# Keeping the split weights of two projections in DRAM between three passes of a hybrid encoder block

## The chip, the cores and the metric

The kernel runs on one core of one Trainium2 chip. The metric is the device time of one execution in microseconds (us). The profile is one further execution, recorded by the hardware profiler.

## The reference

The block handles 1024 tokens of width 1024 in float32. Stick-breaking attention (8 heads of 64) and mLSTM (4 heads of 128) run side by side, their outputs are joined and go through one output projection; then a PEER layer routes each token to 128 of 16384 single-neuron experts through a query projection. Cut to what matters here:

```python
x = x + gate1 * jnp.einsum('bsm,md->bsd', mixed, w_out[l])          # 1024 x 1024 weights
h2 = rms_norm(x, g_norm2[l]) * (1 + scale2) + shift2
# peer(h2, ...)
q = jnp.einsum('bsd,dq->bsq', h, w_q).reshape(b, s_len, 8, 2, 128)   # 1024 x 2048 weights
scores = jnp.einsum('bshpc,hpnc->bshpn', q, sub_keys)
top_s, top_i = lax.top_k(scores, 16)
# pairs of the two top lists, top 16 of them, softmax gate, then
act = gelu(einsum('td,tkd->tk', xb, expert_u[idx]))
y = einsum('tk,tkd->td', gate * act, expert_v[idx])
```

## The kernel before

Tokens are columns. Matrix products that need float32 accuracy use three matmuls of a rounded type (F32R): each operand is split into a high part (ACT copies it with rounding, L121) and a low part (VectorE or POOL subtracts, L125), and `mm3` sums high x high, low x high and high x low (L129 to L131).

`weights` (L257 to L269) makes the two parts of one block of 128 output features, `wh` and `wl`, each 128 x 8 x 128 (0.524 MB), each with two buffers. In the stages considered here it works in four quarters: a load of 128 KB on SP's queue into `wf` (L266, three buffers), an ACT copy into `wh`, a POOL subtraction into `wl`. The output projection has 8 such blocks, the query projection 16.

The tokens are taken in three groups, `GROUPS`: 512, 256 and 256. For each group the output projection (`out_proj`, blocks named `wo`) and the routing (`route`, blocks named `wq`, product tile `pq`) run once, so each weight block is loaded and split three times. Around these, `build` weaves generators together by hand-set step weights:

- attention of the later tokens (`stick_on`, `mlstm`), with keys and values streamed back on SP's queue (`kvrs`, `kvrm`), beside the first output projection, the first routing, the second output projection and the start of the second routing;
- the gate matrix build (`wbuild`, tiles `wo1`, `wo2`, `wm`, `wst`, product `wps`) beside the third output projection and third routing. Its tile `wo` in the rows without a suffix on a VectorE or ACT line L984 to L989 belongs to this build, not to the output projection;
- 24 blocks of the dense expert products made ahead (`ahead`, tiles `uf`, `uh`, `ul`, `da`) from the third routing on.

Last comes the dense phase: 128 expert blocks for 640 tokens on TensorE, woven with row gathers for the other 384 tokens, issued on POOL's queue (tiles `gu`, `gv`, five buffers, L918 and L929).

The weave gives the order in which instructions are written; a scheduler that times the program in a simulation then settles each engine's order. Each engine and each DMA queue works in that order: an instruction that waits holds all behind it.

In DRAM the kernel already keeps intermediate tiles (`mix_d`, `x1_d`, `kvs_d` and others) in the pool `dr`.

Of the kernel before, what the change touches and what calls it, by code (L numbers as in the profile page):

```python
# [8 lines left out]
F32 = mybir.dt.float32  # L9
F32R = mybir.dt.float32r  # L10
# [7 lines left out]
P = 128  # L18
S = 1024
D = 1024  # L20
KB = D // P
# [91 lines left out]
class Kernel:  # L113
# [140 lines left out]
        nc.vector.tensor_mul(y, y, t)  # L254
        return y

    def weights(self, src, name, pool=None):  # L257
        w = pool or self.wp
        wh = w.tile([P, KB, 128], F32R, tag="wh", name=f"wh{name}", bufs=2)
        wl = w.tile([P, KB, 128], F32R, tag="wl", name=f"wl{name}", bufs=2)  # L260

        n, e = (4, "v") if w is self.wp else (2, "g")
        for q in range(KB // n):
            ks = slice(n * q, n * q + n)
            wf = w.tile([P, n, 128], F32, tag="wf", name=f"wf{name}_{q}", bufs=3)
            self.nc.sync.dma_start(wf, src[:, ks])  # L266
            self.split(wf, wh[:, ks], wl[:, ks], "s", e)
        return wh, wl

    def start(self, hp, st):  # L270
# [412 lines left out]
    def out_proj(self, f, w):  # L683

        nc, a, pp = self.nc, self.a, self.pp
        t0, n = GROUPS[f]
        gl = slice(t0, t0 + n)
        mx = self.wide(f, "mx")
        for k in range(KB):
            v = w.tile([P, n], F32, tag="kst", name=f"mx{f}_{k}", bufs=4)  # L690
            nc.sync.dma_start(v, self.mix_d[f][k])
            if k >= 4:
                o = w.tile([P, n], F32, tag="rq", name=f"mo{f}_{k}", bufs=2)
                nc.sync.dma_start(o, self.o_d[k - 4][:, gl])
                nc.vector.tensor_mul(v, v, o)
            self.split(v, mx[0][:, k], mx[1][:, k], "s", "v")
        yield 7
        acc = w.tile([P, n], F32, tag="acc", name=f"acc{f}", bufs=1)
        for i in range(KB):
            wt = self.weights(a["w_out"][i], f"wo{f}_{i}", w)  # L700
            ps = pp.tile([P, H], F32, tag="mm", name=f"op{f}_{i}")[:, :n]
            self.product(ps, wt, mx)
            x1 = w.tile([P, n], F32, tag="kst", name=f"xr{f}_{i}", bufs=4)
            nc.sync.dma_start(x1, a["xT"][:, i, gl])
            nc.vector.scalar_tensor_tensor(out=x1, in0=ps, scalar=self.mod[:, 16 + i : 17 + i], in1=x1, op0=ALU.mult,
                                           op1=ALU.add)
            nc.sync.dma_start(self.x1_d[i][:, gl], x1)
            if i:
                sq = w.tile([P, n], F32, tag="sq", name=f"sqh{f}_{i}", bufs=1)
                nc.scalar.activation(sq, x1, AF.Square)  # L710
                nc.gpsimd.tensor_add(acc, acc, sq)
            else:
                nc.scalar.activation(acc, x1, AF.Square)
            if not f:
                self.to_tokens(i, x1, self.x1t_d, w)
            yield 6
        yield None
        ms = pp.tile([P, H], F32, tag="mm", name=f"msh{f}")[:, :n]
        nc.tensor.matmul(ms, self.mean1024, acc, start=True, stop=True)
        r = self.rsqrt_wide(ms, f"h{f}", n, w, n)  # L720
        h2 = [x[:, :, ND0:] for x in self.da] if f == 1 else self.wide(f, "h2")
        for k in range(KB):
            u = w.tile([P, n], F32, tag="kst", name=f"h2{f}_{k}", bufs=4)
            nc.sync.dma_start(u, self.x1_d[k][:, gl])
            nc.vector.scalar_tensor_tensor(out=u, in0=u, scalar=self.scol2[:, k : k + 1], in1=r, op0=ALU.mult,
                                           op1=ALU.mult)
            sh = self.mod[:, 24 + k : 25 + k]
            self.shifted(u, sh, h2[0][:, k], h2[1][:, k])
            if not f:
                nc.scalar.activation(u, u, AF.Identity, bias=sh)  # L730
                self.to_tokens(k, u, self.h2_d, w)
                nc.sync.dma_start(self.h2e_d[k], u[:, G:])
            yield 5
        self.h2[f] = h2
# [29 lines left out]
    def route(self, f, w):  # L764

        nc, a, pp = self.nc, self.a, self.pp
        n = GROUPS[f][1]
        nt = n // P

        nh = max(1, 4 // nt)  # L770
        for hp in range(16):
            if hp % (2 * nh) == 0:
                top = w.tile([P, nh * nt, 2, 16], F32, tag="top", name=f"top{f}_{hp}", bufs=2)
                tix = w.tile([P, nh * nt, 2, 16], U32, tag="tix", name=f"tix{f}_{hp}", bufs=2)
            r0 = hp // 2 % nh * nt
            nm = f"{f}_{hp}"
            wt = self.weights(a["w_q"][hp], f"wq{f}_{hp}", w)
            sk = w.tile([P, P], F32, tag="sk", name=f"sk{nm}", bufs=2)
            nc.sync.dma_start(sk, a["skT"][:, hp])
            ps = pp.tile([P, H], F32, tag="mm", name=f"pq{nm}")[:, :n]  # L780
            self.product(ps, wt, self.h2[f])
            q = w.tile([P, n], F32, tag="rq", name=f"rq{nm}", bufs=2)
            nc.scalar.copy(q, ps)
            sc = pp.tile([P, H], F32, tag=SC_TAG[f], name=f"sc{nm}")
            for i in range(nt):
                ts = slice(i * P, (i + 1) * P)
                nc.tensor.matmul(sc[:, ts], q[:, ts], sk, start=True, stop=True)
            self.best([sc[:, i * P : (i + 1) * P] for i in range(nt)], [top[:, r0 + i, hp % 2] for i in range(nt)],
                      [tix[:, r0 + i, hp % 2] for i in range(nt)], "mr", nm, w)
            yield 9  # L790
            if hp % 2:
                if r0 + nt == nh * nt:
                    self.level2(f, hp // 2 + 1 - nh, nh, top, tix, w)
                if hp == 15:
                    self.softmax(f, w)
                yield 11
# [298 lines left out]
    def build(self):  # L1095
        tc, nc, ctx, a = self.tc, self.nc, self.ctx, self.a
        self.early_c = ExitStack()
        self.consts()
        pool = lambda n, b, **kw: ctx.enter_context(tc.tile_pool(name=n, bufs=b, **kw))
        dr = pool("dr", 1, space=bass.MemoryType.DRAM)  # L1100
        tiles = lambda nm, n, shape: [dr.tile(shape, F32, name=f"{nm}{i}") for i in range(n)]
        self.o_d, self.mix_d = tiles("o_d", 4, [P, S]), [tiles(f"mix_d{f}_", KB, [P, g[1]]) for f, g in enumerate(GROUPS)]
        self.kvs_d, self.kvm_d = tiles("kvs_d", 4, [P, NT, 2, P]), tiles("kvm_d", 4, [P, NT, 2, P])
# [14 lines left out]
        with ExitStack() as st:  # L1118
            open_ = lambda n: st.enter_context(tc.tile_pool(name=n, bufs=1, reuse_waits="tile"))
            mp = open_("mp")  # L1120
            hp = open_("hp")
# [32 lines left out]
        def queries(u):  # L1154

            return woven(*((chain(*(f(h, u) for h in range(4))), 1) for f in (self.stick_on, self.mlstm)))
# [10 lines left out]
        with right("xw") as xw:  # L1167
            project = lambda f: self.out_proj(f, xw)
            route = lambda f: self.route(f, xw)
            with right("ak3") as self.ak:  # L1170
                q = [queries(1), queries(2)]
                with left("bg") as self.bg:
                    p = project(0)
                    run(woven((chain(upto(p), upto(p)), 95), attend(q[0], CUT[0])))
                    r = route(0)
                    run(woven((islice(r, CUT[1]), 10 * CUT[1]), attend(q[0], 56 - CUT[0])))
                    p = project(1)
                    run(woven((r, 10 * (24 - CUT[1])), (upto(p), 55), attend(q[1], CUT[2])))
                self.da = [enter(left(f"da{x}")).tile([P, KB, ND - 256], F32R, name=f"da{x}") for x in "hl"]
                r = chain(self.early(xw), p, route(1))  # L1180
                run(woven((islice(r, CUT[3] + 9), 10 * CUT[3] + 45), attend(q[1], 72 - CUT[2])))
# [16 lines left out]

            before = ahead()
            run(woven((first(route(2)), 240), (wbs(*W_T[1]), 1.8 * 32 * len(W_T[1])), (islice(before, N_A[0]), 6 * N_A[0])))  # L1200
        self.early_c.close()
        self.wr = enter(right("wr"))
# [74 lines left out]
```

## Time and profile before

| | |
|---|---|
| median of 3 runs | 3305.99 us (3305.73 to 3321.35) |
| the profiled execution | 3304.93 us |
| its span, first to last instruction | 3303.2 us |
| TensorE's mean granted clock in it | 0.961 of full speed |
| busy share of the span | PE 93%, VectorE 82%, ACT 51%, POOL 46% |
| DMA queues by share of 16 engines | SP's queue 35.4%, POOL's queue 34.0% |

PE is TensorE's matmuls, PEld its weight loads, DVE VectorE, POOL GpSimd, SP the engine that issues most DMAs. Matmuls are pipelined and their ends are modelled, so a busy PE is not PE at its peak. "L125" is line 125 of the kernel. Busy shares are means over stages with different limits, so the stages have to be read apart.

### The profile page before, as it was taken

How to read it: one execution, taken by the hardware profiler on the slowest of the kernel's cores; microseconds unless marked ns; L12 is line 12 of the kernel's file. 1: busy time of each engine (PE TensorE's matmuls, PEld its weight loads, DVE VectorE, ACT ScalarE, POOL GpSimd, SP SyncE). 2: the span in 40 equal slices, each digit the busy share in tenths (PEclk: the TensorE clock that was granted, in tenths of full speed). 3: DMA queues.
4: the chain of work that ended last, by engine and by line, in shares of the span. 5: the costliest groups of instructions: out<-in, count | busy, mean ns of one | idle time of the engine just before them, and what ended most of it. 6: DMA issues, size and time to landing. Idle time of an engine off the chain costs nothing.

```text
span 3303.2 us, 53461 instructions
## 1 busy us (share of the span) xinstructions
PE 3060.2 (93%) x18581; PEld 2790.1 (84%) x18581; DVE 2696.0 (82%) x5464; ACT 1678.0 (51%) x3646; POOL 1534.7 (46%) x1334
## 2 busy tenths in 40 slices
PE   6998998988889789999889999999999998999995
PEld 4666676666667679999889999999999998999995
DVE  7776764479988966988679898988888888888997
ACT  4766776774676696789323333333333333333331
POOL 3000003645676434243356565556555555555564
PEclk8999998989989889999999999999999999999998
DMA  5244334532333455398989999999999998899998
GB/s 188 77 131 141 104 89 161 162 114 81 94 115 101 139 192 170 138 333 329 335 302 334 338 326 334 332 341 329 335 314 333 334 315 314 306 339 330 321 333 280
DMA packets 388863, 799.51 MB, mean 242 GB/s; under 512 B 35032, under 2 KB 216792, under 8 KB 386032
## 3 DMA queue, kind: packets, MB, share of 16 engines
q1 hardware_dynamic: 268368, 387.03, 35.4%
q0 software_dynamic: 110624, 402.77, 34.0%
q10 hardware_dynamic: 9600, 6.29, 0.6%
q8 instruction: 146, 2.39, 0.3%
q14 instruction: 125, 1.02, 0.1%
HBM read 716.23 MB, written 79.73 MB: 241 GB/s over the span
## 4 chain that ended last, share of the span: by engine, by line
PE 28%; issue 11%; DVE 11%; DMA 11%; POOL 8%; ACT 4%; SPq 0%; POOLq 0%; DVEq 0%; ACTq 0%
POOL gv L929 4%; PE da L129 4%; PE da L131 4%; PE da L130 4%; DMA vf<-in_V_dram 3%; POOL gu L918 3%; DMA gu<-in_U_dram,idx 2%; PE dy L129 2%; PE dy L130 2%; PE dy L131 2%; PE wps L998 2%; DVE gy L931 2%; PE yr L129 1%; PE yr L130 1%; PE yr L131 1%
## 5 line engine op out<-in xcount | busy, mean ns | idle before, releaser
L918 POOL DMA_INDIRECT gu<-in_U_dram,idx x384 | 521.4, 1358 | 455.9 <-DVE gu L920 373.6
L929 POOL DMA_INDIRECT gv<-in_V_dram,idx x384 | 528.7, 1377 | 367.6 <-DVE gy L931 316.3
L931 DVE SCALAR_TENSOR_TENSOR gy<-gv,gA,gy 128x1024 f32<-128x1024 f32 x384 | 491.1, 1279 | 15.0 <-DMA gv<-in_V_dram,idx 12.5
L920 DVE SCALAR_TENSOR_TENSOR gu<-gu,gh 128x1024 f32<-128x1024 f32 x384 | 460.2, 1220 | 43.0 <-DMA gu<-in_U_dram,idx 38.5
L1092 ACT COPY dt<-dy 128x384 f32<-128x384 f32 x336 | 159.9, 480 | 497.4 <-PE dy L131 425.1
L129 PE MATMUL dy<-dgh,vh 128*128 128x384 f32 x1024 | 345.6, 339 | 18.0 <-ACT dt L1092 18.0
L129 PE MATMUL da<-dah,uh 128*128 128x384 f32 x1024 | 347.5, 339 | 8.9 <-ACT uh L121 6.1
L131 PE MATMUL da<-dah,ul 128*128 128x384 f32 x1024 | 346.7, 339 | 1.1 <-DVE ul L125 1.1
L130 PE MATMUL da<-dal,uh 128*128 128x384 f32 x1024 | 346.8, 339 | 0.0
L130 PE MATMUL dy<-dgl,vh 128*128 128x384 f32 x1024 | 344.9, 337 | 0.0
L131 PE MATMUL dy<-dgh,vl 128*128 128x384 f32 x1024 | 344.1, 337 | 0.0
L129 PE MATMUL yr<-dgh,vh 128*128 128x256 f32 x1024 | 283.3, 285 | 17.1 <-ACT vh L121 15.4
L129 PE MATMUL da<-h2h,uh 128*128 128x256 f32 x1024 | 291.4, 285 | 0.0
L130 PE MATMUL da<-h2l,uh 128*128 128x256 f32 x1024 | 290.9, 284 | 0.0
L131 PE MATMUL da<-h2h,ul 128*128 128x256 f32 x1024 | 290.7, 284 | 0.0
L130 PE MATMUL yr<-dgl,vh 128*128 128x256 f32 x1024 | 287.3, 284 | 0.6 <-DVE dgl L125 0.6
L131 PE MATMUL yr<-dgh,vl 128*128 128x256 f32 x1024 | 281.7, 283 | 0.0
L125 POOL TENSOR_TENSOR vlm<-kvrm,vhm 128x128 fp32r<-128x128 f32 x56 | 31.1, 557 | 448.5 <-ACT vhm L121 438.4
L1093 DVE TENSOR_TENSOR dy<-dy,dt 128x384 f32<-128x384 f32 x336 | 184.6, 553 | 52.1 <-ACT dt L1092 48.4
L125 DVE TENSOR_TENSOR vl<-vf,vh 128x1024 fp32r<-128x1024 f32 x128 | 156.2, 1220 | 84.6 <-ACT vh L121 82.9
L125 POOL TENSOR_TENSOR wlwq<-wfwq,whwq 128x256 fp32r<-128x256 f32 x192 | 149.6, 796 | 135.7 <-ACT whwq L121 130.5
L129 PEld LDWEIGHTS dy<-dgh,vh 128*128 128x128 f32 x1024 | 194.2, 190 | 21.0 <-ACT dt L1092 21.0
(435 smaller groups left out, 8927.1 us busy)
## 6 DMA issues: line engine op xcount, KB each, us to landing
uf<-in_UT_dram SPq DMA_DIRECT2D x128, 512.0 KB
vf<-in_V_dram SPq DMA_DIRECT2D x128, 512.0 KB
w_d<-wst SPq DMA_DIRECT2D x19, 2048.0 KB
dw<-w_d SPq DMA_DIRECT2D x32, 1216.0 KB
wfwq<-in_w_q_dram SPq DMA_DIRECT2D x192, 128.0 KB
wada<-in_w_adaT_dram SPq DMA_DIRECT2D x64, 256.0 KB
wfwo<-in_w_out_dram SPq DMA_DIRECT2D x96, 128.0 KB
wada<-in_w_adaT_dram SPq DMA_DIRECT2D x16, 512.0 KB
```

Of the source, the lines that this page charges most:

```text
L125: e.tensor_sub(lo, src, hi.bitcast(F32))
L129: mm(out, sh, mh, start=start, stop=False, skip_group_check=skip)
L130: mm(out, sh, ml, start=False, stop=False, skip_group_check=skip)
L131: mm(out, sl, mh, start=False, stop=stop, skip_group_check=skip)
L918: nc.gpsimd.indirect_dma_start(out=u, out_offset=None, in_=a["U"], in_offset=bass.IndirectOffsetOnAxis(ap=idx[:, k : k + 1], axis=0))
L920: nc.vector.scalar_tensor_tensor(out=u, in0=u, scalar=1.0, in1=h2, op0=ALU.mult, op1=ALU.mult, accum_out=A[:, k : k + 1])
L929: nc.gpsimd.indirect_dma_start(out=vv, out_offset=None, in_=a["V"], in_offset=bass.IndirectOffsetOnAxis(ap=idx[:, k : k + 1], axis=0))
L931: nc.vector.scalar_tensor_tensor(out=y, in0=vv, scalar=A[:, k : k + 1], in1=y, op0=ALU.mult, op1=ALU.add)
L998: nc.tensor.matmul(ps[:, t], o2[:, t], ms[t], start=True, stop=True)
L1092: nc.scalar.copy(t, ps)
L1093: nc.vector.tensor_add(y[:, i], y[:, i], t)
```

## The change

The first time that a weight block of the output or the query projection is made, both finished parts are also stored to DRAM, in tiles of their own, on SP's queue. In the two later passes the block is not loaded and split again: its two parts are loaded from DRAM straight into `wh` and `wl`, with two transfers of 0.524 MB on POOL's queue. The other users of `weights` pass no name to keep and do as before. The five buffers of the gathers (`GU`) are the same before and after.

```diff
-    def weights(self, src, name, pool=None):
+    def weights(self, src, name, pool=None, keep=None):
+
         w = pool or self.wp
         wh = w.tile([P, KB, 128], F32R, tag="wh", name=f"wh{name}", bufs=2)
         wl = w.tile([P, KB, 128], F32R, tag="wl", name=f"wl{name}", bufs=2)
+        if keep in self.parts_d:
+            for t, d in zip((wh, wl), self.parts_d[keep]):
+                self.nc.gpsimd.dma_start(t, d.bitcast(F32R))
+            return wh, wl
 
         n, e = (4, "v") if w is self.wp else (2, "g")
         for q in range(KB // n):
...
             self.nc.sync.dma_start(wf, src[:, ks])
             self.split(wf, wh[:, ks], wl[:, ks], "s", e)
+        if keep:
+            self.parts_d[keep] = [self.dr.tile([P, KB, 128], F32, name=f"{x}_{keep}") for x in ("kwh", "kwl")]
+            for t, d in zip((wh, wl), self.parts_d[keep]):
+                self.nc.sync.dma_start(d, t.bitcast(F32))
         return wh, wl
...
-            wt = self.weights(a["w_out"][i], f"wo{f}_{i}", w)
+            wt = self.weights(a["w_out"][i], f"wo{f}_{i}", w, f"o{i}")
...
-            wt = self.weights(a["w_q"][hp], f"wq{f}_{hp}", w)
+            wt = self.weights(a["w_q"][hp], f"wq{f}_{hp}", w, f"q{hp}")
...
-        dr = pool("dr", 1, space=bass.MemoryType.DRAM)
+        dr = self.dr = pool("dr", 1, space=bass.MemoryType.DRAM)
+        self.parts_d = {}
```

## Rows read from the trace of the kernel before

**Rows 1.** The page: busy time of each engine, its share of the span, instructions.
```profile
PE 3060.2 (93%) x18581; PEld 2790.1 (84%) x18581; DVE 2696.0 (82%) x5464; ACT 1678.0 (51%) x3646; POOL 1534.7 (46%) x1334
```

**Rows 2.** Windows of two phases: length, engines' busy us, granted clock, DMA share, GB/s.
```profile
535.00:1410.00 875.00, 774.04 (x4261) 631.13 (x4262) 705.23 (x2592) 623.57 (x1661) 451.96 (x517) 0.92 0.43 138
1410.00:3303.00 1893.00, 1816.91 (x12338) 1809.33 (x12336) 1628.78 (x2145) 704.87 (x1309) 1052.36 (x770) 0.98 0.93 325
```

**Rows 3.** Windows by stage, columns as named in the first line.
```profile
core 0: us, PE busy (x) PEld busy (x) DVE busy (x) ACT busy (x) POOL busy (x), PEclk, DMA share, GB/s
550.00:640.00 90.00, 88.98 (x398) 64.75 (x397) 43.13 (x75) 66.89 (x172) 63.61 (x77) 0.99 0.61 186
640.00:880.00 240.00, 206.01 (x904) 149.10 (x904) 214.27 (x954) 146.30 (x364) 119.50 (x136) 0.92 0.33 98
880.00:975.00 95.00, 84.89 (x401) 59.89 (x401) 86.02 (x257) 66.70 (x182) 74.40 (x91) 0.91 0.42 123
975.00:1110.00 135.00, 115.35 (x665) 93.02 (x666) 124.68 (x511) 85.19 (x221) 89.18 (x102) 0.92 0.34 104
1110.00:1160.00 50.00, 38.66 (x230) 36.02 (x230) 45.46 (x128) 44.35 (x129) 18.42 (x18) 0.81 0.45 147
1160.00:1240.00 80.00, 67.15 (x452) 62.06 (x450) 51.91 (x98) 80.00 (x238) 23.14 (x27) 0.89 0.53 193
1240.00:1280.00 40.00, 37.57 (x272) 36.78 (x272) 13.89 (x66) 24.40 (x65) 21.54 (x28) 0.96 0.40 124
1280.00:1350.00 70.00, 67.28 (x502) 66.47 (x501) 62.19 (x265) 47.49 (x134) 31.21 (x32) 0.98 0.53 188
```

**Rows 4.** The chain that ended last, 1160 to 1240 us, its shares by line.
```profile
by line: ACT wm L994 46.9%; ACT wst L999 21.4%; ACT wo L985 7.4%; ACT wo L984 6.8%; ACT whwo L121 4.6%; ACT h2h L308 4.0%; ACT whwq L121 3.0%; issue 2.6%; ACT sqh L710 1.9%; ACT rwyh L248 0.7%; ACT rwth L251 0.6%; ACT rwyh L249 0.4%
```

**Rows 5.** The same chain, 975 to 1110 us.
```profile
by line: DMA wfwq<-in_w_q_dram 12.6%; issue 5.4%; POOL wlwq L125 4.4%; DVE L L507 4.1%; PE pq L130 3.5%; DVE mr L809 3.4%; PE pq L129 3.4%; PE pq L131 3.2%; PE sc L787 3.1%; DVE xs L895 2.7%; PE y L138 2.4%; DVE top L805 2.3%; DVE tix L807 
```

**Rows 6.** The same chain, 1240 to 1280 us: shares, then pieces (start, us).
```profile
by line: DMA wfwq<-in_w_q_dram 35.3%; POOL wlwq L125 13.5%; ACT whwq L121 7.6%; PE da L129 6.7%; PE da L130 6.5%; PE da L131 6.0%; issue 4.6%; PE sc L787 4.2%; PE wps L998 2.9%; PE pq L129 2.6%; PE pq L130 2.6%; ACT uh L121 2.4%; PE pq L131
...
1254.12 2.33 DMA wfwq<-in_w_q_dram
...
1266.45 2.74 DMA wfwq<-in_w_q_dram
...
1274.04 2.15 DMA wfwq<-in_w_q_dram
```

**Rows 7.** Groups of instructions, 535 to 1410 us: busy us, mean ns; idle before them.
```profile
L125 POOL TENSOR_TENSOR wlwq<-wfwq,whwq 128x256 fp32r<-128x256 f32 x192 | 149.6, 796 | 135.7 <-ACT whwq L121 130.5 <-PE wps L998 4.8
...
L125 POOL TENSOR_TENSOR wlwo<-wfwo,whwo 128x256 fp32r<-128x256 f32 x96 | 81.3, 861 | 61.9 <-ACT whwo L121 40.3 <-PE wps L998 19.7 <-PE op L131 0.7
L121 ACT CAST whwq<-wfwq 128x256 fp32r<-128x256 f32 x192 | 73.2, 409 | 63.1 <-DMA wfwq<-in_w_q_dram 49.9 <-PE pq L130 9.6 <-PE op L130 2.3
...
L121 ACT CAST whwo<-wfwo 128x256 fp32r<-128x256 f32 x96 | 36.7, 406 | 24.9 <-DMA wfwo<-in_w_out_dram 22.2 <-PE op L130 1.9 <-issue 0.5
```

**Rows 8.** Windows of tile wfwo (two rows), then wfwq: ACT, POOL busy us.
```profile
1110.00:1160.00 50.00, 5.30 (x14) 11.31 (x14) 0.81 0.45 147
1160.00:1240.00 80.00, 4.64 (x12) 13.32 (x14) 0.89 0.53 193
...
1160.00:1240.00 80.00, 3.33 (x8) 6.14 (x8) 0.89 0.53 193
```

**Rows 9.** Issues by POOL, whole span: ns min/median/max of one.
```profile
L918 POOL DMA_INDIRECT gu<-in_U_dram,idx x384: 932/1312/1990, 1411.8 to 2987.4; - x192
...
L1049 POOL DMA_DIRECT2D dw<-we_d x1: 606/606/606, 1589.8 to 1589.8; - x1
```

**Rows 10.** Issues of the query weights by SP's queue, ns min/median/max.
```profile
L266 SPq DMA_DIRECT2D wfwq<-in_w_q_dram x192: 327/328/1546, 618.8 to 1341.5; - x192
```

**Rows 11.** The chain, 1410 to 1440 us: one load of 0.524 MB.
```profile
1423.43 4.41 DMA uf<-in_UT_dram
```

**Rows 12.** Windows of tile pq, the second routing: PE, PEld, ACT busy us.
```profile
975.00:1110.00 135.00, 64.42 (x384) 54.90 (x384) 5.85 (x16) 0.92 0.34 104
```

## The prediction

> **What bounds the kernel now.** I read the busy line first [rows 1], then the windows of two long phases [rows 2]. After 1410 us the dense phase holds TensorE at 1816.91 of 1893 us and the DMA engines at 0.93; nothing that the diff touches runs there, so it moves as a block, earlier or later by whatever the stretch before it gains or loses. Between 535 and 1410 us no engine is full on average (PE 774 of 875, DVE 705, ACT 624, POOL 452), so the same phase has to be cut by stage [rows 3]. There the limit changes hands: PE is at 88.98 of 90 us in the first output projection (550 to 640), DVE at 214 of 240 in the first routing (640 to 880), DVE again at 124.68 of 135 in the second routing (975 to 1110), ACT at exactly 80.00 of 80 in the stretch where the third output projection ends beside the gate-matrix build (1160 to 1240), PE at 37.57 of 40 and 67.28 of 70 in the third routing. The chain of waits says what the limit means. From 1160 to 1240 almost all of it is ACT [rows 4]. From 975 to 1110 the load of a weight quarter takes 12.6% and its POOL subtraction 4.4% [rows 5]. From 1240 to 1280 load, subtraction and ACT copy take 35.3, 13.5 and 7.6% [rows 6]: the ring of three `wf` buffers turns there, each quarter waiting 2.2 to 2.7 us for its load and then for ACT and POOL, while PE fills the time with dense blocks.
>
> **What the change takes away.** The output projection has 8 weights and the query projection 16, each used in three passes. Each use now makes four quarters, so 96 and 192 ACT copies, as many POOL subtractions and as many loads. Passes 2 and 3 lose theirs: 64 + 128 = 192 of each. By the groups [rows 7] two thirds of 73.2 + 36.7 us is 73 us off ACT, and two thirds of 149.6 + 81.3 us is 154 us off POOL; 192 issues of 0.328 us are 63 us off SP's queue [rows 10]. An engine's relief counts only where that engine, or the ring through it, ends last, so I go by stage.
>
> 1160 to 1240: ACT has no idle time and the chain is ACT, so each copy counts. The copies there are 4.64 + 3.33 = 7.97 us [rows 8]: 8 us. 1110 to 1160: ACT is at 44.35 of 50 us beside a DVE at 45.46, with 5.30 us of copies [rows 3, 8]; bounds 0 and 5.3, I take 2, since two engines are nearly level. Together 10.
>
> 975 to 1110: the ring's share is (12.6 + 4.4)% of 135 = 23 us, the upper bound [rows 5]. DVE is idle for 135 - 124.68 = 10.3 us only [rows 3], and it is not relieved; I take half of that idle time, 5. 1240 to 1280: upper bound (35.3 + 13.5 + 7.6)% of 40 = 22.6 us, but PE's idle time there is 2.4 us and its work stays; I take 3, a little over the idle time because PE's busy time is modelled and holds some waiting. 880 to 975 (DVE idle 9 us, no row of the ring on top) and 1280 to 1350 (PE idle 2.7 us): 1 each, bounds 0 and the idle time. The gains sum to 10 + 5 + 3 + 2 = 20 us; with all the upper bounds, 13.3 + 23 + 22.6 + 9 + 2.7 = 71, with the lower ones 0.
>
> **What it adds: stores.** In pass 1 each weight's two tiles, 0.524 MB each, go back to DRAM: 16 stores in the first output projection and 32 in the first routing, all on SP's queue, each behind the last ACT copy or POOL subtraction of its weight. Queued behind a store on SP are the next weight's quarters, the streamed keys and values, `xr` and the stores of x1. In 550 to 640 the engines move 186 GB/s at a share of 0.61 [rows 3], that is 305 GB/s when busy. The 8.4 MB there need 27.5 us of engine time and 0.39 x 90 = 35 us are free: it fits, at about nine tenths full. A load issued behind one weight's pair of stores is late by up to 1.05 MB / 305 GB/s = 3.4 us. If each of 8 weights lost that, 27 us; if none, 0. PE is busy for 99% of that stage, so the loads run ahead of it now; I take 4. In the first routing the upper bound is 16 x 3.4 = 55 us, but DMA is at 0.33 and DVE sets the pace with 15 us for each weight; a quarter late by 3.4 us is not late for the product after the current one: 0. Without that cover 25.7 us of DVE idle time would be the first thing to grow. The 48 issues of about 0.33 us [rows 10] are 16 us of SP time over 330 us and hide there.
>
> **What it adds: loads on POOL's queue.** Passes 2 and 3 issue 96 transfers of 0.524 MB from POOL. The trace has one plain transfer from POOL, 0.606 us for 64 KB, and gathers of the same 128 rows of 4 KB at 0.932, 1.312 and 1.990 us (least, median, most) [rows 9]. That is 58 to 191 us of POOL; I take the median, 126 us, so POOL ends some 28 us lighter (at the ends 96 lighter and 37 heavier), and at 452 of 875 us it is no bound either way [rows 2]. What matters is lateness. A tile can be refilled only when the product two back has released it. Before, a refill is ready for its first rows one ACT copy and one subtraction later, about 0.41 + 0.80 us [rows 7], because the quarters lie in SBUF already. Now both tiles have to be issued and to land: 2 x 1.31 + 4.41 us (a 0.524 MB load from SP, [rows 11]) = 7.0 us; with the least issue and a 2.33 us landing [rows 6] it is 4.2, with the greatest issue 8.4. In the second routing 384 matmuls, 16 products, take 135 us, 8.4 us each, of which PE works 64.42 / 16 = 4.0 us [rows 12]. Two buffers must turn in 7.0 + 4.0 = 11 us for two products and have 16.9: 5.9 us to spare, so I take 0, with an upper bound in the rivals. The waits on POOL's queue have behind them the subtractions of stick-breaking and mLSTM, for which PE waits; but before, the same tiles' subtractions stood in that place and waited on ACT.
>
> At this place a rule speaks against the change. The gathers' spread shows that an issue from POOL can take twice its least time [rows 9], while SP's issues are mostly at 0.328 us [rows 10]. The Trainium skill, SBUF — State Buffer, section "Who interferes with whom", says that descriptors for a DMA issued from GpSimd are written by GpSimd through a port that VectorE takes whole in its two-port modes, and advises the SP or ACT queue instead. No row here shows a DMA held that way. By that rule the issue would stand nearer 1.99 us, and the loop of two products nearer 12.4 us than 11.0, still under 16.9; the sum would stay as it is and the chance of the fifth case below would rise.
>
> **Sum.** -20 + 4 = -16 us on the profiled execution's own 3304.93 us: 3288.9. The median of the runs is 3305.99, 1.06 above it, so about 3290. About 0.5% (16.5 us) is what a measurement of this kernel can tell from no change; the forecast lies at that edge. The scheduler orders the queues from its own timing of the new program, so neighbours of the change may shift by some us that I can't price.
>
> **The rivals.** (1) Forecast, -16, own range 3277 to 3302: chance 0.38. (2) The ring was the real pace of the two later routings, and PE's and DVE's busy time hides waiting: 10 + 14 + 12 + 3 - 4 = 35 us faster, some three fifths of both ring bounds, 3271. For it: 56% of the chain from 1240 to 1280 [rows 6]; against: PE at 37.57 of 40 beside it. Chance 0.16. (3) Hidden anyway: behind ACT the next engine takes over at once, PE with 67.15 of 80 us at a granted clock of 0.89, and the loads' own wait takes the ring's place: about -3, 3303. For it: 44.35 and 45.46 us beside each other in 1110 to 1160. Chance 0.18. (4) The stores push the first output projection out by most of its bound, 24 of 27 us: -20 + 24 = +4, 3310. Against: PE at 99% there now, which leaves room only if the weights are ahead. Chance 0.08. (5) Slower: the parts come late in passes 2 and 3. The place is POOL's in-order queue, where a refill stands behind a subtraction that waits for ACT. It decides when a refill is ready later than 16.9 - 4.0 = 12.9 us after its release, 5.9 us more than I reckon. If half of the 48 weights lose 1.6 us beyond the gains, 38 - 16 = +22, 3328; the casting load from DRAM into the rounded type, which no row prices, could do it too. The rule above is on this side. Chance 0.20. That the parts are not kept, or are made again, the diff excludes: the dictionary is filled in pass 1 and both later passes use the same names.
>
> **From cases to numbers.** Faster by over 0.5%: 0.45 of case 1, all of case 2: 0.17 + 0.16 = 0.33. Slower by over 0.5%: case 5 and a little of 4: 0.22. Within 0.5%: 0.45. The range of 8 in 10 leaves out half of case 2 and half of case 5: 3270 to 3325.
>
> **What would show it.** The ACT copies, subtractions and loads of the two weights at a third of their counts; ACT below full from 1160 to 1240 and that stretch some 8 us shorter; first output projection longer by under 8 us, with its DMA share near 0.9; first routing unchanged; POOL's loads landing within 5 us; PE in the second routing rarely waiting for a load of kept parts. I am wrong if PE waits for those loads by tens of us, if the first projection grows by 20, or if the dense phase itself changes length.

## The result and the profile after

The changed kernel took 3284.01 us (median of 7 runs, 3272.23 to 3301.17) against 3305.73 us for the kernel before (7 runs): ratio 0.9937, 95% interval 0.9908 to 0.9966, that is 0.34 to 0.92% faster. Measured a second time it came out at 0.9917 (0.9891 to 0.9943). The profiled execution took 3280.11 us with a span of 3278.3; before 3304.93 and 3303.2.

First the groups of instructions of the changed kernel from 535 to 1410 us, which answer to [rows 7] (columns as there):
```profile
L125 POOL TENSOR_TENSOR wlwq<-wfwq,whwq 128x256 fp32r<-128x256 f32 x64 | 48.8, 781 | 36.9 <-ACT whwq L121 34.0 <-ACT zs L512 1.6 <-PE Sm L138 1.1
L125 POOL TENSOR_TENSOR wlwo<-wfwo,whwo 128x256 fp32r<-128x256 f32 x32 | 26.6, 842 | 8.6 <-ACT whwo L121 8.4
L121 ACT CAST whwq<-wfwq 128x256 fp32r<-128x256 f32 x64 | 23.1, 400 | 29.4 <-PE pq L130 15.2 <-DMA wfwq<-in_w_q_dram 10.1 <-PE op L130 3.9
L121 ACT CAST whwo<-wfwo 128x256 fp32r<-128x256 f32 x32 | 12.5, 401 | 4.6 <-DMA wfwo<-in_w_out_dram 4.6
```
The counts are a third of what they were, and 74 us of ACT and 156 us of POOL are gone. The windows of its stages answer to [rows 3]; the stages end at other times now, so the borders are its own:
```profile
550.00:650.00 100.00, 95.61 (x407) 69.81 (x406) 47.62 (x85) 72.72 (x186) 66.35 (x78) 0.94 0.82 273
650.00:880.00 230.00, 196.72 (x891) 144.62 (x890) 202.85 (x934) 139.67 (x346) 112.43 (x128) 0.94 0.52 167
880.00:975.00 95.00, 80.66 (x414) 59.03 (x412) 90.89 (x274) 59.15 (x155) 62.21 (x79) 0.96 0.60 187
975.00:1094.00 119.00, 105.30 (x646) 83.75 (x643) 108.81 (x476) 67.23 (x160) 56.65 (x69) 0.97 0.54 164
1094.00:1164.00 70.00, 60.49 (x413) 56.63 (x413) 65.44 (x181) 58.51 (x170) 23.11 (x25) 0.88 0.80 274
1164.00:1240.00 76.00, 65.66 (x451) 61.84 (x450) 42.58 (x152) 51.35 (x145) 9.29 (x17) 0.91 0.59 205
1240.00:1330.00 90.00, 90.00 (x705) 89.38 (x705) 75.37 (x285) 66.27 (x186) 15.65 (x18) 1.00 0.70 244
```
The first projection (550 to 650) has its DMA share at 0.82 instead of 0.61. The third (1094 to 1164) takes 70 us, with DVE at 65.44 of 70 in it and PE at 90.00 of 90 later on. That none of these rows has ACT full is due to their borders. From 1107 to 1194 us ACT is as full as it was before, although it no longer copies any of these weights there (in the second profile 76.20 of 80 us from 1110 to 1190):
```profile
1107.00:1194.00 87.00, 76.92 (x528) 71.28 (x527) 74.18 (x170) 86.49 (x253) 21.51 (x25) 0.91 0.69 246
```
The chain of waits from 1110 to 1164 us, which answers to [rows 4], shows what it holds now, as shares and two pieces ("issue" is time in which an engine waited for nothing that the profile shows):
```profile
by line: issue 36.8%; DMA wlwo<-kwl_o 26.0%; ACT wm L1003 10.8%; PE op L131 6.2%; ACT wst L1008 6.0%; PE wps L1007 5.8%; PE op L129 5.5%; PE op L130 5.0%; ACT wo L994 2.5%; ACT wo L993 1.9%; ACT sqh L719 1.1%; POOL whwo L264 0.9%; POOLq L26
...
1124.96 4.93 DMA wlwo<-kwl_o
1134.23 9.12 DMA wlwo<-kwl_o
```
A kept tile lands 4.9 to 9.1 us after its issue there, and one in the third routing (the chain from 1164 to 1240 us) lands after 11.53:
```profile
1198.40 11.53 DMA wlwq<-kwl_q
```
POOL's issues of them (min/median/max, ns) answer to [rows 9]:
```profile
L264 POOL DMA_DIRECT2D whwq<-kwh_q x32: 530/570/593, 953.2 to 1310.1; - x32
L264 POOL DMA_DIRECT2D wlwq<-kwl_q x32: 530/537/557, 953.7 to 1310.7; - x32
L264 POOL DMA_DIRECT2D whwo<-kwh_o x16: 530/593/756, 848.3 to 1150.6; - x16
L264 POOL DMA_DIRECT2D wlwo<-kwl_o x16: 530/537/571, 849.0 to 1151.2; - x16
```
The best view for a change that touches many stages is a table of milestones: the start of the last high x high matmul of each projection and routing, and of the first resident product (`yr`) of the dense phase, in one profiled execution of each kernel (us from the span's start). The last two columns are the span and what remains of it after `yr` starts. Here are the experiments' rows too:

| kernel | proj. 1 | rout. 1 | proj. 2 | rout. 2 | proj. 3 | rout. 3 | dense | span | dense length |
|---|---|---|---|---|---|---|---|---|---|
| before | 638.3 | 925.6 | 954.1 | 1101.8 | 1197.7 | 1358.0 | 1614.7 | 3303.2 | 1688.5 |
| before, again (e9) | 639.8 | 927.0 | 955.0 | 1102.2 | 1197.9 | 1354.8 | 1611.8 | 3295.3 | 1683.5 |
| changed | 649.5 | 926.1 | 955.0 | 1094.4 | 1164.2 | 1330.1 | 1584.9 | 3278.3 | 1693.4 |
| changed, again (e10) | 644.2 | 926.6 | 954.4 | 1098.1 | 1170.8 | 1334.4 | 1587.8 | 3286.6 | 1698.8 |
| e1 output parts only | 647.9 | 928.9 | 954.9 | 1108.3 | 1176.9 | 1347.8 | 1600.3 | 3286.2 | 1685.9 |
| e2 query parts only | 640.7 | 922.7 | 959.6 | 1100.4 | 1200.5 | 1350.9 | 1608.8 | 3324.8 | 1716.0 |
| e3 stores only | 644.8 | 927.6 | 961.8 | 1106.4 | 1198.8 | 1357.9 | 1615.5 | 3304.5 | 1689.0 |
| e4 loads only | 640.7 | 924.5 | 949.6 | 1089.5 | 1162.3 | 1322.7 | 1575.1 | 3278.3 | 1703.2 |
| e5 no ACT, proj. 3 | 640.7 | 928.2 | 956.3 | 1104.7 | 1193.5 | 1356.5 | 1614.4 | 3315.9 | 1701.5 |
| e6 six buffers | 634.1 | 923.5 | 945.0 | 1101.3 | 1172.2 | 1343.3 | 1597.5 | 3306.1 | 1708.6 |
| e7 no ACT, wider | 643.4 | 930.9 | 977.4 | 1114.7 | 1209.1 | 1373.8 | 1634.6 | 3339.8 | 1705.2 |
| e8 loads on SP | 640.9 | 918.4 | 946.2 | 1078.1 | 1150.6 | 1314.0 | 1565.2 | 3264.8 | 1699.6 |
| e11 stores on ACT | 646.7 | 937.6 | 968.9 | 1104.2 | 1179.4 | 1348.6 | 1603.6 | 3304.9 | 1701.3 |
| e12 SP, six buffers | 643.6 | 932.1 | 959.5 | 1097.1 | 1159.7 | 1325.9 | 1586.1 | 3291.6 | 1705.5 |

The changed kernel is level with before up to the second projection, 7 us ahead after the second routing, 33 after the third projection, 28 after the third routing and 30 at the dense phase. Five of these 30 are lost again inside the dense phase.

### The profile page after: what moved, and what is told of

Its sections match the earlier page's. It is cut to its first block, busy times and chain, and to the rows that moved or that the text cites. A ratio compares the mean times of both kernels' runs of the same rounds, so it can differ in the third digit from the quotient of the medians.

```text
span 3278.3 us, 52849 instructions
## 1 busy us (share of the span) xinstructions
PE 3040.6 (93%) x18581; PEld 2780.0 (85%) x18581; DVE 2679.3 (82%) x5464; ACT 1616.6 (49%) x3454; POOL 1444.4 (44%) x1238
## 4 chain that ended last, share of the span: by engine, by line
PE 61%; DVE 14%; DMA 10%; issue 7%; ACT 4%; POOL 3%; SPq 1%; POOLq 0%; DVEq 0%; ACTq 0%
PE da L130 7%; PE da L131 7%; PE da L129 7%; PE wps L1007 4%; PE dy L129 4%; PE dy L130 4%; PE dy L131 4%; DMA vf<-in_V_dram 3%; PE yr L129 2%; PE yr L130 2%; PE yr L131 2%; POOL gv L938 2%; DMA gv<-in_V_dram,idx 2%; POOL gu L927 1%; PE z L503 1%
## 5 line engine op out<-in xcount | busy, mean ns | idle before, releaser
L129 PE MATMUL dy<-dgh,vh 128*128 128x384 f32 x1024 | 345.3, 339 | 14.4 <-ACT dt L1101 14.4
L121 ACT CAST vh<-vf 128x1024 fp32r<-128x1024 f32 x128 | 134.3, 1049 | 163.2 <-DMA vf<-in_V_dram 159.4
L129 PEld LDWEIGHTS yr<-dgh,vh 128*128 128x128 f32 x1024 | 194.6, 193 | 21.9 <-ACT vh L121 21.5
```

What stands on the lines that cost most here:

```text
L121: nc.scalar.copy(hi, src)
L129: mm(out, sh, mh, start=start, stop=False, skip_group_check=skip)
```

## The experiments

My theory (A) was the prediction's: ACT is full beside the third projection, and its copies are what the change takes away there. Against it stood (B) the ring of three quarter buffers, (C, E) the scheduler's new order, and (D) stores that are never taken back.

**e1 and e2: one projection's parts at a time.** e1 passes no name to keep from the routing, e2 none from the output projection:
```diff
-            wt = self.weights(a["w_q"][hp], f"wq{f}_{hp}", w, f"q{hp}")     # e1
+            wt = self.weights(a["w_q"][hp], f"wq{f}_{hp}", w)
-            wt = self.weights(a["w_out"][i], f"wo{f}_{i}", w, f"o{i}")      # e2
+            wt = self.weights(a["w_out"][i], f"wo{f}_{i}", w)
```


> Only the output projection's parts are kept; the query projection makes its parts three times as before. Theory A (the gain lies in the third output projection, where ACT is full and its 32 copies go): nearly the whole gain of the change, 18 to 28 us faster than before, with the third output projection's last matmul some 25 us earlier against the second routing's last one, and nothing gained in the second routing. Rival B (the ring of quarter buffers was the pace of the routings): under 8 us faster. Rival C (the scheduler's new order, not an engine's relief): no telling, but the stage times need not add up to the change's.

> Only the query projection's parts are kept. Theory A: 0 to 8 us faster, all of it in the second routing (about 7 us shorter), the third output projection at its old 94 us. Rival B: 15 us faster or more, in both later routings. Rival C: a third output projection that changes by over 10 us although nothing in it was touched.

e1: 0.9981 (0.9959 to 1.0003), median 3298.22. e2: 1.006 (1.0037 to 1.0084), slower, median 3325.07. At the dense phase the two add up to two thirds, 14.4 + 5.9 = 20 us early against 30: the third projection is short with the output parts (68.6 us after the second routing, against 95.9 before) and is not without them (100.1). At the end they don't add up at all: e2 loses 27 us in a dense phase of 1716.0 us whose code nobody touched. Theory A expected 18 to 28 us from e1 and 0 to 8 from e2, and the medians gave 5 and -21. Its sizes fail for the whole; its stage is the right one.

**e3 and e4: stores alone, loads alone.** e3 drops the branch that loads kept parts. e4 drops the stores and loads both parts from the weights themselves:
```diff
-        if keep in self.parts_d:                                   # e3
...
-        if keep:
+        if keep and keep not in self.parts_d:
...
-                self.nc.gpsimd.dma_start(t, d.bitcast(F32R))       # e4
+                self.nc.gpsimd.dma_start(t, src.bitcast(F32R))
...
+            self.parts_d[keep] = (src, src)
```


> The parts are made three times as before, and in the first pass also stored, but never loaded: the stores alone. Theory A: the first output projection ends 5 to 12 us later, the first routing, paced by VectorE, takes it back, and the whole is within 5 us of before. Rival D (stores are never taken back): 7 to 20 us slower. The stores cost nothing anywhere if the first output projection ends where it did.

> No stores; in the second and third pass both parts are loaded by POOL's queue from the weights themselves, so the low part holds the weight instead of the remainder and the results differ: the loads and the relief alone. Theory A: as fast as the change or up to 8 us faster, 20 to 30 us faster than before, since the stores are hidden. Rival D: 30 us faster or more.

e3: 1.0058 (1.0038 to 1.0078), median 3323.11, so by the timed runs stores alone cost some 19 us, as D expects. Its profile does not show where: the first projection ends 6.5 us late, the first routing 2.0, and the dense phase starts 0.8 late and is as long as before. But the profiled execution, at 3306.23 us, was the fastest of its 8 runs. e4: 0.994 (0.9917 to 0.9962), as fast as the change and 20.5 us faster than before, as A expected (20 to 30) and D did not (30 or more). Its dense phase starts 39.6 us early, 10 more than with the stores, and takes 1703.2 us, 15 more than before.

**e5 and e7: ACT's relief without the rest.** VectorE makes the high parts, in the third projection alone (e5) or in both later projections and the third routing (e7):
```diff
-            wt = self.weights(a["w_out"][i], f"wo{f}_{i}", w)
+            wt = self.weights(a["w_out"][i], f"wo{f}_{i}", w, "v" if f == 2 else "s")     # e5
...
-            self.split(wf, wh[:, ks], wl[:, ks], "s", e)
+            self.split(wf, wh[:, ks], wl[:, ks], hi, e)
```


> The kernel before, but in the third output projection alone VectorE makes the high parts instead of ACT; loads, quarter buffers and POOL's subtractions stay. Theory A (ACT's relief): the third output projection takes 67 to 80 us instead of 94, and the first resident product of the dense phase starts 12 to 26 us earlier. Rival B (the ring of load, copy and subtraction, or POOL's place in it): under 8 us shorter. Theory E (the scheduler writes another order for the dense phase, whose code is untouched, and its length follows that order): the planned order of the dense phase here is that of the kernel that keeps the query parts alone, so the dense phase takes 1700 to 1716 us instead of 1688 and eats most of the gain.

> The kernel before, but VectorE makes the high parts in the second and third output projection and in the third routing; the second routing, where VectorE is nearly full, stays. Theory A: third output projection 67 to 80 us, start of the dense phase 15 to 30 us earlier. Rival B: under 8. Theory E: the planned order of the dense phase is that of the changed kernel, so it takes 1686 to 1700 us and the whole is 10 to 25 us faster than before.

e5: 1.0072 (1.0047 to 1.0098), e7: 1.0091 (1.0061 to 1.0122), both slower. In e5 the third projection ends 88.8 us after the second routing, 7 less than before, and the dense phase starts where it did. In its window of that stage ACT is far from full, and the stage is hardly shorter (columns as in [rows 3]; below it SP's wait for the ring: total, times, longest):
```profile
1105.00:1194.00 89.00, 65.49 (x430) 61.65 (x430) 78.34 (x207) 64.00 (x183) 45.69 (x41) 0.83 0.48 160
```
```profile
SPq L266 <- POOL wlwo L125: 31.9, 19, 8.8
```
SP still waits 31.9 us for a POOL subtraction to free a quarter buffer. Theory A, that the time of ACT's copies sets this stage, does not stand; VectorE has its own load there, so the test is not clean in size. In e7 the third projection ends 94.4 us after the second routing, hardly less than before, and e7 is 23 us late at the end of the second projection. Of these, 18 were lost since the end of the first routing, in a stretch where VectorE was at 86 of 95 us already [rows 3]. Theory E's dense lengths came out for e5 (1701.5, 1700 to 1716 expected) and not for e7 (1705.2, 1686 to 1700 expected).

**e6: the ring alone.** Six quarter buffers instead of three; every copy, subtraction and load stays:
```diff
-            wf = w.tile([P, n, 128], F32, tag="wf", name=f"wf{name}_{q}", bufs=3)
+            wf = w.tile([P, n, 128], F32, tag="wf", name=f"wf{name}_{q}", bufs=3 if w is self.wp else 6)
```


> The kernel before with six quarter buffers instead of three in these stages; all copies and subtractions stay. Theory A: third output projection within 8 us of its 94, start of the dense phase within 8 us of before. Rival B: third output projection shorter by 15 us or more, second routing by 5 or more. Theory E: the planned order is again that of the kernel that keeps the query parts alone, so the dense phase takes 1700 to 1716 us and the whole is 10 to 28 us slower than the start of the dense phase alone would make it.

1.0015 (0.9996 to 1.0034), median 3305.97: no change in the whole. But the third projection ends 70.9 us after the second routing, as in the changed kernel (69.8), with all of ACT's copies in place. The third projection's matmuls (first and last start), the window of that stage and SP's wait for the ring, in the kernel before and then in e6:
```profile
L129 PE MATMUL op<-mxh,whwo x64: 276/284/579, 1103.8 to 1197.7; 128*128 128x256 f32 x64
```
```profile
1102.00:1198.00 96.00, 74.98 (x490) 69.11 (x490) 77.48 (x199) 84.34 (x248) 39.42 (x39) 0.88 0.55 187
```
```profile
SPq L266 <- POOL wlwo L125: 31.8, 23, 6.8
```
```profile
L129 PE MATMUL op<-mxh,whwo x64: 276/280/582, 1106.1 to 1172.2; 128*128 128x256 f32 x64
```
```profile
1101.00:1172.00 71.00, 55.06 (x363) 50.57 (x361) 63.57 (x170) 56.03 (x165) 37.76 (x39) 0.86 0.51 165
```
```profile
SPq L266 <- POOL wlwo L125: 11.4, 17, 2.1
```
So 25 us of this stage go without one copy taken off ACT: three buffers are fewer than the four quarters of a block, and the ring turned too slowly, as theory B said for the routings. For the routings B is not borne out: it expected the second one shorter by 5 us or more, and that one ended where it did (1101.3 against 1101.8), although the second projection had ended 9 us earlier.

Two things limit this reading. ACT is not out of the loop, since POOL's subtractions wait for its copies, and the copies stand in ACT's order among the build's instructions. In the kernel before, three quarters issued at 1111.76 to 1113.17 us were copied at 1131.91; the rows show SP's issues, ACT's copies and POOL's wait in that stage:
```profile
1111.76 0.85 SPq L266 DMA_DIRECT2D wfwo<-in_w_out_dram  x2
...
1113.17 0.38 SPq L266 DMA_DIRECT2D wfwo<-in_w_out_dram  x1
```
```profile
1131.91 1.03 ACT L121 CAST whwo<-wfwo 128x256 fp32r<-128x256 f32 x3
```
```profile
POOL wlwo L125 <- ACT whwo L121: 25.1, 10, 4.8
```
And part of the 25 us is work moved on: PE runs 363 matmuls in e6's stage against 490, of which the projection's 192 are the same, so less of the gate-matrix build runs beside it. Whether the build only fills the time of a slow ring, or slows the ring by standing before its copies, is not separated, because six buffers also change the order that the scheduler writes. Then 11 of the 25 us are given back in the third routing (171.1 us instead of 160.3), and the dense phase, longer by 20 as theory E expected, takes the rest: 17.2 us early at its start, nothing at the end.

**e8, e11, e12: other queues.** e8 loads the kept parts on SP's queue, e12 adds the six buffers to that, e11 stores on ACT's queue:
```diff
-                self.nc.gpsimd.dma_start(t, d.bitcast(F32R))
+                self.nc.sync.dma_start(t.bitcast(F32), d)          # e8, e12
-                self.nc.sync.dma_start(d, t.bitcast(F32))
+                self.nc.scalar.dma_start(d, t.bitcast(F32))        # e11
```


> The changed kernel with the loads of the kept parts on SP's queue instead of POOL's. If POOL's queue costs something (issues held, work queued behind a refill that waits for PE), the two later routings and the third output projection get 5 to 15 us shorter together and the dense phase starts that much earlier than the changed kernel's. If the waits only move to SP's queue, in front of the streamed keys and values, it starts 0 to 15 us later. Theory E: the planned order of the dense phase is one of its own, so its length can be anything between 1686 and 1716 us.

> The changed kernel with the stores on ACT's queue instead of SP's; loads on POOL's queue as before. If what the stores cost is their place in SP's queue in front of the quarter loads, the first output projection ends 5 us earlier or more than the changed kernel's 650. If it is the DMA engines' load, it ends within 3 us of it. If ACT now stands waiting for POOL's last subtraction of each weight, the first output projection or the first routing ends 5 to 20 us later.

> The changed kernel with the kept parts loaded on SP's queue and six quarter buffers: the two edits that shortened the stretch before the dense phase, together. Ring theory: only the first pass still uses the ring, so the first output projection shortens by 3 to 9 us, the first routing, paced by VectorE, keeps most of that back, and the dense phase starts 0 to 8 us earlier than with the SP loads alone (1565). The whole 20 to 35 us faster than before, depending on the dense phase's length.

e8: 0.9927 (0.9904 to 0.995), median 3278.24; its interval overlaps both of the changed kernel's, so it is not shown to be faster. Its dense phase starts 20 to 23 us earlier (5 to 15 were expected), 49.5 before that of the kernel before. Five of these are there when the second projection starts (858.8 us against 864.2), before a kept part has been used, so the queue's cost in the later stages is at most some 15 to 18. POOL's waits in the changed kernel (total, times, longest) suggest it:
```profile
POOL big L903 <- DVE hit L900: 100.8, 16, 29.3
POOL whwq L264 <- PE pq L131: 91.8, 18, 15.2
POOL whwq L264 <- PE pq L130: 30.9, 2, 29.7
POOL Ll L125 <- ACT Lh L121: 29.5, 15, 4.9
POOL whwo L264 <- PE op L130: 18.9, 1, 18.9
...
POOL whwo L264 <- PE op L131: 10.9, 4, 3.9
```
For 153 us POOL stands at a refill that waits for PE, with everything behind it in its queue. In e8 such waits stand on SP's queue instead (68.9 us for `pq`, 20.2 for `wps`), and the stages are shorter all the same. e11: 0.9978 (0.996 to 0.9996); the first projection ends at 646.7, between the changed kernel's two profiles (649.5 and 644.2), as expected if the DMA engines' load is what the stores cost. The first routing ends 11 us later. That ACT waits for POOL's last subtraction was the reason put forward, and its trace does not bear it out: from 550 to 940 us ACT waits for POOL's subtractions of weights for 1.2 us only. e12: 0.996 (0.9941 to 0.9979), 15 us faster where 20 to 35 were expected, with a dense phase that starts 21 us later than e8's: the two edits do not add.

**e9 and e10: both kernels again.** No edit.

> The kernel before, unchanged, profiled once more: how far stage times and the dense phase repeat. If the stages up to the dense phase are set by the program, each milestone (last matmul of each projection and routing, first resident product) comes within 3 us of the first profile. If the dense phase's length is set by the program's order (Theory E) it is again 1685 to 1693 us; if it is set by each execution's own luck in DMA, it may be 10 us or more off.

> The changed kernel, unchanged, profiled once more beside the kernel before on the same chip: the ratio again within 0.9908 to 0.9966, milestones within 3 us of the first profile, start of the dense phase about 30 us earlier than before's. Dense phase by Theory E 1690 to 1697 us again; by each execution's luck, 10 us or more off.

Ratios 0.9982 (0.9964 to 1.0) and 0.9917. The first is the same program against itself, so a few tenths of a per cent are noise here. Milestones repeat within 3.2 us in the kernel before and 6.6 in the changed one, the dense lengths within 5.0 and 5.4. Theory E expected 1690 to 1697 and 1685 to 1693, and got 1698.8 and 1683.5: just outside on both sides. The 33 us between kernels are far more, but two profiles are two executions, and the 12 runs of e9 went from 3289.92 to 3312.89 us.

## Why the prediction was right, and where not

The forecast was 16 us faster, and the medians moved by 21.7. The sum fits; two of its steps do not, and that it fits is in part luck: the third projection gave 16 us more than forecast, the third routing 10 less, and the dense phase took 5 back.

**What goes** was right: 192 copies and 192 subtractions, 74 us of ACT (73 reckoned) and 156 of POOL (154).

**The stretch 1110 to 1240** (10 us) is the step that failed. "ACT has no idle time and the chain is ACT, so each copy counts" priced the stretch by the copies' own time on ACT. The third projection became 26 us shorter (23 in the second pair of profiles). Taking its copies off ACT gave 7 (e5) or 1.5 (e7); turning the ring with six buffers and all copies in place gave 25 (e6). ACT at 80.00 of 80 was mostly the gate-matrix build [rows 4], and ACT is at 86.49 of 87 in the changed kernel, with the copies gone. The ring that I gave to the routings [rows 5, 6] had its largest price here. Because build work moves between the two stages, the fairer sum runs from the second routing's end to the third's: 256.2 us before, 242.0 with six buffers, 235.7 with the change and 251.8 with ACT relieved (e5). By it the change gave 20.5 us (16.3 in the second pair), six buffers 14 and ACT's relief 4. That the ring, rather than the order in which the scheduler put the build, is the cause is argued from e5 and e6 and not shown by itself.

**Second routing** (5): 8.3 us shorter, 3.5 in the second pair; right. **Third routing** (4): it became 5.6 and 6.7 us longer, with part of the build that used to run beside the third projection (PE runs 413 matmuls there instead of 490), on a PE at 90.00 of 90. **Second projection** (1): level.

**Stores** (+4): the first projection ends 11.2 and 4.4 us later in the two pairs, and by the end of the first routing nothing is left (+0.5 and -0.4), as forecast; VectorE, at 202.85 of 230 us from 650 to 880, would cover them. That this is their whole cost is not shown: e3's runs are slower by 19 us, e4's dense phase starts 10 us earlier without them.

**Loads** (0): a POOL issue took 0.53 to 0.59 us, not the 1.31 reckoned from gathers; landing took 4.9 to 11.5 us in the chain's pieces, not 4.41 nor within 5. PE waited little for them in all: from 880 us on, PE's weight loads waited 5.4 + 1.8 + 1.1 + 1.0 = 9.3 us, shown here with total, times, longest:
```profile
PEld pq L131 <- DMA wlwq<-kwl_q: 5.4, 2, 5.2
...
PEld op L131 <- DMA wlwo<-kwl_o: 1.8, 4, 0.8
PEld op L129 <- DMA whwo<-kwh_o: 1.1, 2, 0.8
...
PEld pq L129 <- DMA whwq<-kwh_q: 1.0, 1, 1.0
```
The case of late parts (5) did not come about. The rule of the Trainium skill, SBUF — State Buffer, "Who interferes with whom", by which VectorE's two-port modes hold such issues, is not seen in their times (median 537 to 593 ns, most 756), with VectorE at 65.44 of 70 us; no row tells how many of VectorE's instructions run in such a mode. The same loads from SP's queue in e8 land after 3.1 to 9.7 us, which three pieces of 4.93, 9.12 and 11.53 us do not tell apart:
```profile
DMA to landing us min/median/max: 3.1/4.7/9.7
```
e8, which follows the advice, starts its dense phase 20 us earlier, but by the rows above POOL's issues waited for PE, which the rule does not speak of.

**"It moves as a block"** is the other step that failed. The dense phase started 29.8 us early and ended 24.9 early; in the second pair 24.0 and 8.7. Its length is 1684 to 1689 us in the kernel before and 1693 to 1699 in the changed one. That the dense phase changes length was one of the prediction's own signs of being wrong. What sets the length stays open. The scheduler does write its order anew, also where no code changed: of the changed kernel's 1553 VectorE instructions from the first dense subtraction on, the longest sequence that stands in the same order (buffer numbers left out) has 1462 in the kernel before and 1370 in e2. All four kernels near e2's order (e2 itself, and e4, e5, e6 with 1470 to 1498 of its 1552) took 1701 to 1716 us there; but those with the changed kernel's order or nearly so (e1, e3, e7, e11, with 1536 to 1553) spread from 1686 to 1705, so the order alone does not explain the profiles.

Each profile is one execution, though, and the executions of one program spread by 14 to 33 us here. An estimate for the median execution is the profile's dense length plus the median time less the profiled execution's time, if the earlier stages repeat as they did in the two pairs. It gives 1689 and 1690 us for the kernel before, 1697 and 1691 for the changed one, 1695 to 1697 for e1, e7 and e11, and 1706 to 1715 for e2, e4, e5 and e6. That fits the order, except for e3 with 1706, whose dense phase started 0.8 us from that of the kernel before. By the same estimate the changed kernel's dense phase is longer by 1 to 8 us. No experiment changed that order alone.

## What to carry to other kernels

An engine at 100% in a stage and all over its chain may be filling its time with other work: before crediting the relief of one kind of its instructions, double the buffers of the loop that they stand in, which costs one line, and see whether the stage shortens with them in place. Compare kernels by milestones, not by the end alone: here kernels that had won 11 to 17 us before the last phase (e1, e6, e11) ended 17 us faster to 3 us slower than before, in their profiles. A phase whose code is untouched need not be constant when a scheduler orders the program again; leave a per cent for it in the range, and do not read its length off one profile when the runs spread by more than the difference.

## What the runs showed that I had not expected

A plain DMA of 0.524 MB from POOL holds POOL for no longer (0.530 to 0.593 us as a rule) than one of 64 KB did [rows 9]. The landing of such loads differs: 4.93 us and 9.12 us within ten microseconds, in a stage where the DMA share is 0.80; why is not shown. VectorE's copies of a quarter took less than ACT's, 371 ns in e5's third projection against 406 on average over all three before [rows 7]. POOL's subtractions beside them had a mean of 1021 ns, but one of 5.3 us lifts it: their median was 736, against 780 in the same stage before.
```profile
L125 POOL TENSOR_TENSOR wlwo<-wfwo,whwo 128x256 fp32r<-128x256 f32 x30 | 30.2, 1021 | 34.2 <-DVE whwo L123 22.0 <-PE op L131 8.0 <-DMA wfwo<-in_w_out_dram 4.0
...
L123 DVE CAST whwo<-wfwo 128x256 fp32r<-128x256 f32 x29 | 10.4, 371 | 3.0 <-DMA wfwo<-in_w_out_dram 2.4 <-PE op L130 0.5
```
```profile
L125 POOL TENSOR_TENSOR wlwo<-wfwo,whwo x30: 718/736/5257, 1105.1 to 1190.6; 128x256 fp32r<-128x256 f32 x30
```
